# Layer norms on VectorE alone, summed in pairs, and the MLP's gate as a task of its own, in a two-layer decoder step

## The chip, the core and the metric

The kernel runs on one core of a Trainium2 chip. A core has five engines with a queue each: TensorE (PE in the profile; its weight loads are PEld), VectorE (DVE), ScalarE (ACT), GpSimd (POOL) and SyncE (SP), and 16 DMA engines that move data between HBM and the core's memory (SBUF). TensorE writes into eight banks of an accumulator memory (PSUM). The metric is the device time of one execution in microseconds (us); less is better.

## The reference, cut to what matters

One inference step through two decoder layers, for a prompt of 1024 tokens and eight samples of four tokens each: 1056 tokens of 1024 features, all in fp32. Each layer has a mixer (pooling and retention in the first layer, latent attention with a paged cache in the second) and a gated MLP; each of the four is followed by a layer norm over the residual sum. The change touches the norm and the MLP:

```python
def layer_norm(x, g, b):
    mu = jnp.mean(xf, axis=-1, keepdims=True)
    var = jnp.mean(jnp.square(xf - mu), axis=-1, keepdims=True)
    return (xf - mu) * lax.rsqrt(var + LN_EPS) * g + b

def conv_ffn(x, hist, w_up, conv_w, conv_b, w_down):
    h = x @ w_up                         # 1024 -> 2 * 2816
    a, b = h[..., :D_FF], h[..., D_FF:]
    a_ext = jnp.concatenate([hist, a], axis=1)
    conv = conv_b
    for j in range(3):
        conv = conv + conv_w[j] * a_ext[:, j:j + L]
    return (jax.nn.silu(conv) * b) @ w_down, a_ext[:, L:]

# per layer
xp = layer_norm(ALPHA * xp + mixer(xp), ln_mix_g, ln_mix_b)
xp = layer_norm(ALPHA * xp + conv_ffn(xp), ln_ffn_g, ln_ffn_b)
```

## The kernel before, in words

**Layout.** Features lie on the 128 partitions, tokens along the free axis. The residual `z` is [128, 8, 1056]: eight rows of 128 features each. The 1056 tokens are worked in three chunks of 352 (`CHUNKS`); the very last stage has four chunks of 352, 288, 256 and 160 (`ENDS`).

**Matrix products.** A product in fp32 is made of three faster ones. Each operand is split into a high part (a cast to fp32r, on ScalarE) and a low part (the operand less its high part): for weights `wh` and `wl`, 128x1024 elements a unit, for activations `xh` and `xl` (x in the profile), for the gate's result `ah` and `al`. `mm3` multiplies high with high, high with low and low with high. A block (`block`) is one output tile of 128 features by one chunk: eight times `mm3`, 24 matmuls, into one bank.

**Weights.** `open_weights` starts two tasks: one loads raw weights from the SP queue into two buffers (`wr`), the other cuts them into four pairs of buffers (`wh`, `wl`). The low half is written by the engine that `pick` chooses out of the unit's list: before, VectorE and GpSimd for nearly all units (`ffn_units`, `out_units`, `mla_units`).

**The layer norm** (`layer_norm`, from line 743) runs once per chunk, thirteen times in all. It sums the eight rows of z, takes the mean over the partitions with one fp32 matmul by a matrix of 1/1024 (`self.mean`), has ScalarE copy the mean from its bank (`ln_m`), subtracts it from two rows at a time, squares (ScalarE, `ln_q`, one row at a time), sums the squares (`ln_v`), takes their mean in the same way, then root (ScalarE), reciprocal (VectorE, `ln_r`), and for each pair of rows multiply, scale and shift (ScalarE or VectorE), high part (ScalarE or VectorE) and low part. For some chunks TensorE does a sum itself with eight matmuls (`SUM1`, `SUM2`, `END1`, `END2`: the last chunk's sum, and in the last stage also the squares of the last two). The steps that a local function `op` issues go to VectorE or GpSimd, whichever the planner believes will finish first, with 1000 ns in VectorE's favour (`LNX`).

**The MLP** (`ffn`): 22 features of 128, in phases (`SIZES`). For each feature and chunk there is a block for the first half (`first`: ScalarE copies it into the row buffer `a`, one of two) and one for the second (`second`: three VectorE steps of the convolution into `y`, Silu on ScalarE, a multiply with the block's bank into `g`, then `split` into `ah` and `al`). `down` multiplies a phase's features by the down weights and adds into z. In the first phase (`head`) the blocks follow chunk by chunk: all four of chunk 0, then chunk 1, then chunk 2, each as the norm before it gets done.

**What sets the order.** Everything is written as Python generators (tasks) with priorities, run by a planner (`Pipe.run`) that keeps estimated clocks of the engines (`Clocks`). A task yields what it waits for: an event, a buffer, data that must be ready (`rd`), or that VectorE's clock is at most 1 us ahead (`lag`). At each step the planner takes the first task by priority whose wait has ended at TensorE's estimated time. Norms have priority 0, the MLP 10, the output projection's blocks 10 to 17 (`out_proj`, `one`, which also adds the block to z after it). The order in which the tasks issue instructions becomes their rank; a scheduler behind it then builds each engine's queue, in which an instruction of lower rank can go ahead of one that is not ready by that scheduler's estimate. Each queue is then worked strictly in its order.

All engine calls pass through one recording helper, so that most lines of the profile are 405 (the other engines), 616 (`mm`), 632 (`tile`) and 638 (`tr`).

Of the kernel before, what the change touches and what calls it, by code (L numbers as in the profile page):

```python
# [7 lines left out]
F32 = mybir.dt.float32  # L8
# [48 lines left out]
LNX = -1000.0  # L57
SX = 400.0
HX = 0.0
# [502 lines left out]
class Kernel:  # L562
# [180 lines left out]
    def layer_norm(self, c, g, b, event, final=None, chunks=CHUNKS):  # L743
# [13 lines left out]
        for k in range(8):  # L757
# [3 lines left out]
            if c in sum1:  # L761
                if pm is None:
                    pm = yield from self.bank()
                yield ("rd", z[:, k])
                self.mm(pm[:, :n], self.mean, z[:, k], k == 0, k == 7)
            elif k:
                if s1 is None:
                    s1 = self.ln.tile([128, n], F32, tag="ln_s", name="ln_s", bufs=2)
                op(s1, z[:, 0] if k == 1 else s1, z[:, k], ALU.add)
        if pm is None:  # L770
            yield ("rd", s1)
            pm = yield from self.bank()
            self.mm(pm[:, :n], self.mean, s1, True, True)
        mc = self.ln.tile([128, n], F32, tag="ln_r", name="ln_m", bufs=2)
        nc.scalar.copy(mc, pm[:, :n])
        self.drop()
        prev = pv = None
        for i in range(0, 8, 2):
            op(z[:, i:i + 2], z[:, i:i + 2], wide(mc), ALU.subtract)
            for k in range(i, i + 2):  # L780
                sq = self.ln.tile([128, n], F32, tag="ln_q", name="ln_q", bufs=2)
                nc.scalar.activation(sq, z[:, k], AF.Square)
                if c in sum2:
                    if pv is None:
                        pv = yield from self.bank()
                    yield ("rd", sq)
                    self.mm(pv[:, :n], self.mean, sq, k == 0, k == 7)
                else:
                    if k == 0:
                        s2 = self.ln.tile([128, n], F32, tag="ln_s", name="ln_v", bufs=2)  # L790
# [8 lines left out]
        rs = self.ln.tile([128, n], F32, tag="ln_r", name="ln_r", bufs=2)  # L799
        nc.scalar.activation(rs, pv[:, :n], AF.Sqrt, bias=self.eps[:, 0:1])  # L800
        nc.vector.reciprocal(rs, rs)
        self.drop()
        for i in range(0, 8, 2):
            yield ("lag", "dve")
            zz = z[:, i:i + 2]
            op(zz, zz, wide(rs), ALU.mult)
            for k in range(i, i + 2):
# [4 lines left out]
            if final is None:  # L812
                hi = self.xh[:, i:i + 2, t0:t0 + n]
                if self.soonest([zz], {"act": 94.0 + n / 0.6, "dve": HX + 70.0 + n / 0.96}, (nc.scalar, nc.vector)) is nc.scalar:
                    nc.scalar.copy(hi, zz)
                else:
                    nc.vector.tensor_copy(hi, zz)
                op(self.xl[:, i:i + 2, t0:t0 + n], zz, hi.bitcast(F32), ALU.subtract)
            else:
                final(c, i, i + 2)  # L820
        pipe.give("ln", at=pipe.now)
# [55 lines left out]
    def ffn_units(self, l):  # L877
        both = (self.nc.vector, self.nc.gpsimd)
# [18 lines left out]
    def ffn(self, l, src, ln, event, final=None):  # L897
# [28 lines left out]
        def second(f, c, ps):  # L926
# [12 lines left out]
            nc.scalar.activation(y[:, :w], y[:, :w], AF.Silu)  # L939
            g = fp.tile([128, CH], F32, tag="g", name="g")  # L940
# [107 lines left out]
    def out_units(self, key, src):  # L1048
        both = (self.nc.vector, self.nc.gpsimd)
# [965 lines left out]
```

## Time and profile before

| | us |
|---|---|
| median of 3 runs | 2903.41 (2899.09 to 2904.54) |
| profiled execution, its own time | 2902.8 |
| its span, first to last instruction | 2901.0 |
| TensorE busy in the span | 2743.6 |
| mean granted TensorE clock | 0.97 |

The stages, from the span's start: retention and pooling to about 341 us, the output projection to about 445, the first MLP to about 1240, latent attention's projections to about 1412, its attention to about 1966, its output projection to about 2072, the second MLP to the end. The norms lie at the seams, around 395 to 495, 1180 to 1260, 2030 to 2123, and 2808 to the end.

How to read the rows: a timeline row has start, duration, engine, line, operation, output<-inputs, shape (partitions x elements), how many are merged, and in brackets the idle time of the engine before it and what released it. A row of waits has the total, the number of times and the longest. A group row has busy time, mean ns of one, and the idle time before. The granted clock is a share of TensorE's full speed.

### The profile page before, as it was taken

Reading aid. Unit: us, or ns where it says so; the run is one execution under the profiler, and the core shown is the slowest. Engines: PE = TensorE matmul, PEld = TensorE weight load, DVE = VectorE, ACT = ScalarE, POOL = GpSimd, SP = SyncE. Lnnn points to the kernel's source line nnn. Section 1 sums busy time; section 2 is a strip of 40 time slices with the busy share of each in tenths; the row PEclk is TensorE's granted clock in tenths of the full one; section 3 lists DMA queues with packets and bytes.
Section 4 is the critical chain, followed back from the end, with each engine's and each line's share of the span. In section 5 each row is a group of like instructions: output and inputs, shape, how many; then the busy total and the mean of one; then the engine's idle time right before and its main releaser. Section 6 shows DMA issues by size and latency. Waiting matters only on the chain.

```text
span 2901.0 us, 43639 instructions
## 1 busy us (share of the span) xinstructions
PE 2743.6 (95%) x16897; PEld 2459.3 (85%) x16897; DVE 1417.1 (49%) x2721; ACT 867.5 (30%) x1831; POOL 850.1 (29%) x884
## 2 busy tenths in 40 slices
PE   8999998999999999989888989799899999999997
PEld 6777997999999999879745555469789999999996
DVE  4444547544444444774343535355764444444455
ACT  3323435211211222243233433243431211211223
POOL 1222334010110010333577777643410110011112
PEclk9999999999999999999999999899999999999997
DMA  3111420211111111132888999874211111111101
GB/s 137 60 56 50 118 80 23 65 44 37 59 44 38 58 44 52 38 100 67 254 293 280 310 318 314 274 236 140 66 44 37 59 44 33 63 45 46 49 25 60
DMA packets 127055, 301.78 MB, mean 104 GB/s; under 512 B 20960, under 2 KB 71952, under 8 KB 126720
## 3 DMA queue, kind: packets, MB, share of 16 engines
q1 hardware_dynamic: 75648, 159.62, 16.9%
q0 software_dynamic: 32576, 113.73, 11.5%
q10 hardware_dynamic: 18624, 25.63, 3.0%
q8 instruction: 134, 2.20, 0.3%
q14 instruction: 73, 0.60, 0.1%
HBM read 283.71 MB, written 15.21 MB: 103 GB/s over the span
## 4 chain that ended last, share of the span: by engine, by line
PE 77%; DMA 6%; DVE 5%; issue 5%; POOL 4%; ACT 2%; SPq 0%; POOLq 0%; DVEq 0%; ACTq 0%
PE bank L616 70%; PE bank L632 3%; DMA kt<-in_kT,kix 3%; DMA vt<-in_vrow,vix 2%; PE sc L616 2%; POOL kt L405 2%; PE bank L638 1%; DVE x L405 1%; DVE ln_v L405 1%; DVE z L405 1%; POOL z L405 1%; DMA p<-qpd 1%; DVE wl L405 1%; DMA kt<-in_kT 1%; POOL vt L405 0%
## 5 line engine op out<-in xcount | busy, mean ns | idle before, releaser
L616 PE MATMUL bank<-x,wh 128*128 128x352 f32 x5664 | 1379.7, 326 | 18.1 <-DVE x L405 16.6
L616 PEld LDWEIGHTS bank<-x,wh 128*128 128x128 f32 x5664 | 992.8, 190 | 32.7 <-DVE x L405 21.7
L616 PE MATMUL bank<-x,wl 128*128 128x352 f32 x2832 | 915.7, 324 | 9.4 <-DVE wl L405 9.4
L616 PEld LDWEIGHTS bank<-x,wl 128*128 128x128 f32 x2832 | 537.1, 190 | 11.1 <-DVE wl L405 10.6
L405 ACT CAST wh<-wr 128x1024 fp32r<-128x1024 f32 (+1 forms) x196 | 202.7, 1041 | 669.9 <-PE bank L616 638.6
L405 DVE SCALAR_TENSOR_TENSOR z<-z,bank 128x352 f32<-128x352 f32 (+3 forms) x440 | 219.6, 511 | 325.6 <-PE bank L616 319.6
L616 PE MATMUL bank<-ah,wh 128*128 128x352 f32 (+3 forms) x1088 | 352.8, 324 | 0.0
L616 PE MATMUL bank<-ah,wl 128*128 128x352 f32 (+3 forms) x1088 | 350.3, 322 | 0.0
L616 PE MATMUL bank<-al,wh 128*128 128x352 f32 (+3 forms) x1088 | 350.2, 322 | 0.0
L405 POOL TENSOR_TENSOR wl<-wr,wh 128x1024 fp32r<-128x1024 f32 (+1 forms) x60 | 145.3, 2430 | 638.3 <-PE bank L616 391.6
L405 POOL DMA_INDIRECT kt<-in_kT,kix x256 | 252.1, 985 | 84.3 <-issue 59.9
L405 DVE TENSOR_TENSOR wl<-wr,wh 128x1024 fp32r<-128x1024 f32 (+1 forms) x138 | 176.9, 1284 | 147.9 <-ACT wh L405 143.3
L616 PE MATMUL bank<-wh,x 128*128 128x512 f32 (+3 forms) x720 | 238.7, 393 | 8.1 <-ACT wh L405 8.1
L616 PEld LDWEIGHTS bank<-ah,wh 128*128 128x128 f32 x1088 | 207.6, 191 | 1.3 <-issue 0.2
L616 PEld LDWEIGHTS bank<-al,wh 128*128 128x128 f32 x1088 | 207.4, 191 | 1.4 <-issue 0.2
L616 PEld LDWEIGHTS bank<-ah,wl 128*128 128x128 f32 x1088 | 207.5, 191 | 0.6 <-DVE wl L405 0.6
L405 POOL COPY co<-a 128x2 f32<-128x2 f32 x44 | 39.2, 892 | 553.9 <-ACT a L405 553.9
L405 DVE SCALAR_TENSOR_TENSOR y<-a,prm,y 128x352 f32<-128x352 f32 (+1 forms) x264 | 166.1, 629 | 9.8
L405 DVE TENSOR_TENSOR g<-y,bank 128x352 f32<-128x352 f32 (+2 forms) x176 | 71.5, 427 | 202.2 <-PE bank L616 201.1
L405 DVE TENSOR_SCALAR y<-a,prm 128x352 f32<-128x352 f32 x132 | 77.0, 583 | 183.6 <-ACT a L405 178.1
L616 PEld LDWEIGHTS bank<-wh,x 128*128 128x128 f32 (+1 forms) x720 | 127.6, 181 | 32.5 <-ACT wh L405 8.1
L405 POOL DMA_INDIRECT vt<-in_vrow,vix x128 | 125.8, 983 | 72.8 <-PE bank L632 28.1
(234 smaller groups left out, 3184.4 us busy)
## 6 DMA issues: line engine op xcount, KB each, us to landing
wr<-in_w_up SPq DMA_DIRECT2D x88, 512.0 KB
kt<-in_kT SPq DMA_DIRECT2D x256, 160.0 KB
wr<-in_w_dn SPq DMA_DIRECT2D x44, 512.0 KB
wr<-in_w_h SPq DMA_DIRECT2D x16, 512.0 KB
wr<-in_w_oe SPq DMA_DIRECT2D x16, 512.0 KB
wr<-in_w_om SPq DMA_DIRECT2D x16, 512.0 KB
z<-in_xT SPq DMA_DIRECT2D x12, 352.0 KB
z<-in_xT ACTq DMA_DIRECT2D x3, 1408.0 KB
```

What stands on the lines that cost most here:

```text
L405: r = f(*args, **kw)
L616: self.nc.tensor.matmul(out, lhsT, rhs, start=start, stop=stop)
L632: self.nc.tensor.matmul(out[32 * g:32 * g + m], lhsT, rhs, start=start, stop=stop, tile_position=(0, 32 * g))
L638: self.nc.tensor.transpose(out, in_, self.ident[:in_.shape[0], :in_.shape[0]])
```

## The change

In the norm, sums run over pairs of rows (tiles of [128, 2, n], one pair added to the next), so that the two halves of a pair are added by two accumulating matmuls with `self.mean`. The subtraction reads the mean straight from the bank; the copy `ln_m` is gone. Squares are taken two rows at a time, and the adds of squares come one pair later. All these steps, and multiply and low part, are VectorE's; the high part is always ScalarE's; the low part of a pair is issued after the next pair's multiply. The low halves of weights, other than the first mixer's and two units that GpSimd cuts whole, are VectorE's. In the MLP, `second` becomes a task of priority 3 that waits for the Silu and for the cast before it issues the next VectorE step; a feature's first block waits until the gate of the feature two before it is done.

```diff
@@ layer_norm
-        both = (nc.vector, nc.gpsimd)
-
-        def op(out, x, y, alu):
-            w = int(np.prod(out.shape[1:]))
-            self.pick(both, w, x, y, more=LNX).tensor_tensor(out, x, y, alu)
+        op = nc.vector.tensor_tensor
...
-            elif k:
+            elif k > 1 and k % 2:
                 if s1 is None:
-                    s1 = self.ln.tile([128, n], F32, tag="ln_s", name="ln_s", bufs=2)
-                op(s1, z[:, 0] if k == 1 else s1, z[:, k], ALU.add)
+                    s1 = self.ln.tile([128, 2, n], F32, tag="ln_s", name="ln_s", bufs=3)
+                op(s1, z[:, 0:2] if k == 3 else s1, z[:, k - 1:k + 1], ALU.add)
         if pm is None:
             yield ("rd", s1)
             pm = yield from self.bank()
-            self.mm(pm[:, :n], self.mean, s1, True, True)
-        mc = self.ln.tile([128, n], F32, tag="ln_r", name="ln_m", bufs=2)
-        nc.scalar.copy(mc, pm[:, :n])
-        self.drop()
+            for a in range(2):
+                self.mm(pm[:, :n], self.mean, s1[:, a], a == 0, a == 1)
         prev = pv = None
+        sqs = []
         for i in range(0, 8, 2):
-            op(z[:, i:i + 2], z[:, i:i + 2], wide(mc), ALU.subtract)
-            for k in range(i, i + 2):
-                sq = self.ln.tile([128, n], F32, tag="ln_q", name="ln_q", bufs=2)
-                nc.scalar.activation(sq, z[:, k], AF.Square)
-                if c in sum2:
...
-                    else:
-                        op(s2, prev, sq, ALU.add)
-                    prev = s2 if k else sq
+            op(z[:, i:i + 2], z[:, i:i + 2], wide(pm[:, :n]), ALU.subtract)
+            if len(sqs) == 2:
+                op(sqs[1], sqs[0], sqs[1], ALU.add)
+                del sqs[0]
+            if i == 6:
+                self.drop()
+            sq = self.ln.tile([128, 2, n], F32, tag="ln_s", name="ln_q", bufs=3)
+            nc.scalar.activation(sq, z[:, i:i + 2], AF.Square)
+            if c in sum2:
...
+                for a in range(2):
+                    self.mm(pv[:, :n], self.mean, sq[:, a], i + a == 0, i + a == 7)
+            else:
+                sqs.append(sq)
             yield ("lag", "dve")
         if pv is None:
-            yield ("rd", s2)
+            op(sq, sqs[0], sq, ALU.add)
+            yield ("rd", sq)
             pv = yield from self.bank()
-            self.mm(pv[:, :n], self.mean, s2, True, True)
+            for a in range(2):
+                self.mm(pv[:, :n], self.mean, sq[:, a], a == 0, a == 1)
...
+        low = []
         for i in range(0, 8, 2):
             yield ("lag", "dve")
             zz = z[:, i:i + 2]
             op(zz, zz, wide(rs), ALU.mult)
+            if low:
+                op(*low.pop())
...
-                if self.soonest([zz], {"act": 94.0 + n / 0.6, "dve": HX + 70.0 + n / 0.96}, (nc.scalar, nc.vector)) is nc.scalar:
-                    nc.scalar.copy(hi, zz)
-                else:
-                    nc.vector.tensor_copy(hi, zz)
-                op(self.xl[:, i:i + 2, t0:t0 + n], zz, hi.bitcast(F32), ALU.subtract)
+                nc.scalar.copy(hi, zz)
+                low.append((self.xl[:, i:i + 2, t0:t0 + n], zz, hi.bitcast(F32), ALU.subtract))
@@ ffn_units, out_units and mla_units alike
-        both = (self.nc.vector, self.nc.gpsimd)
+        both = (self.nc.vector,)
@@ ffn: second
             nc.scalar.activation(y[:, :w], y[:, :w], AF.Silu)
+            yield ("rd", y)
...
-            self.split(ah[:, t0:t0 + n], al[:, t0:t0 + n], g)
+            nc.scalar.copy(ah[:, t0:t0 + n], g)
+            yield ("rd", ah[:, t0:t0 + n])
+            nc.vector.tensor_tensor(al[:, t0:t0 + n], g, ah[:, t0:t0 + n].bitcast(F32), ALU.subtract)
             self.pipe.fire(("act", l, f, c))
@@ ffn: piece
             u = yield from self.unit(("up", l, f, j))
+            if j == 0 and c == 0 and f > 1:
+                yield ("ev", ("act", l, f - 2, 2))
             ps = yield from self.block(u, ks, c, xs)
-            (first, second)[j](f, c, ps)
+            if j:
+                self.pipe.add(second(f, c, ps), 3)
+            else:
+                first(f, c, ps)
```

More of the change, by code (lines that the diff above doesn't have):

```diff
@@ L772, in layer_norm @@
             pm = yield from self.bank()
-            self.mm(pm[:, :n], self.mean, s1, True, True)
-        mc = self.ln.tile([128, n], F32, tag="ln_r", name="ln_m", bufs=2)
-        nc.scalar.copy(mc, pm[:, :n])
-        self.drop()
+            for a in range(2):
+                self.mm(pm[:, :n], self.mean, s1[:, a], a == 0, a == 1)
         prev = pv = None
+        sqs = []
         for i in range(0, 8, 2):
-            op(z[:, i:i + 2], z[:, i:i + 2], wide(mc), ALU.subtract)
-            for k in range(i, i + 2):
-                sq = self.ln.tile([128, n], F32, tag="ln_q", name="ln_q", bufs=2)
-                nc.scalar.activation(sq, z[:, k], AF.Square)
-                if c in sum2:
[L784 to L787, printed above, removed]
-                else:
-                    if k == 0:
-                        s2 = self.ln.tile([128, n], F32, tag="ln_s", name="ln_v", bufs=2)
-                    else:
-                        op(s2, prev, sq, ALU.add)
-                    prev = s2 if k else sq
+            op(z[:, i:i + 2], z[:, i:i + 2], wide(pm[:, :n]), ALU.subtract)
[7 more added lines that the diff above has]
+            if c in sum2:
+                if pv is None:
+                    pv = yield from self.bank()
+                yield ("rd", sq)
[3 more added lines that the diff above has]
+                sqs.append(sq)
@@ L794, in layer_norm @@
             yield ("lag", "dve")
         if pv is None:
-            yield ("rd", s2)
+            op(sq, sqs[0], sq, ALU.add)
+            yield ("rd", sq)
             pv = yield from self.bank()
-            self.mm(pv[:, :n], self.mean, s2, True, True)
-        rs = self.ln.tile([128, n], F32, tag="ln_r", name="ln_r", bufs=2)
+            for a in range(2):
+                self.mm(pv[:, :n], self.mean, sq[:, a], a == 0, a == 1)
+        rs = self.ln.tile([128, n], F32, tag="ln_r", name="ln_r", bufs=1)
@@ L813, in layer_norm @@
                 hi = self.xh[:, i:i + 2, t0:t0 + n]
-                if self.soonest([zz], {"act": 94.0 + n / 0.6, "dve": HX + 70.0 + n / 0.96}, (nc.scalar, nc.vector)) is nc.scalar:
-                    nc.scalar.copy(hi, zz)
-                else:
-                    nc.vector.tensor_copy(hi, zz)
-                op(self.xl[:, i:i + 2, t0:t0 + n], zz, hi.bitcast(F32), ALU.subtract)
+                nc.scalar.copy(hi, zz)
+                low.append((self.xl[:, i:i + 2, t0:t0 + n], zz, hi.bitcast(F32), ALU.subtract))
             else:
                 final(c, i, i + 2)
+        if low:
+            op(*low.pop())
         pipe.give("ln", at=pipe.now)
@@ L1048, in out_units @@
     def out_units(self, key, src):
-        both = (self.nc.vector, self.nc.gpsimd)
+        both = (self.nc.vector,)
         return [((key, p, ob), src[ob], 1024, both) for p in range(2) for ob in range(8)]
@@ L1283, in mla_units @@
         io = self.io
-        e = (self.nc.vector, self.nc.gpsimd)
+        e = (self.nc.vector,)
         out = [(("dq", i), io["w_dq"][i], 1024, e) for i in range(4)]
```

2 lines of the change are left out of this document (removed).

## The prediction, made before the changed kernel was run

> **What bounds the kernel now.** I read the page's first part, then a table of stretches, then the list of waits of TensorE, then the timelines around the largest waits.
>
> ```profile
> PE 2743.6 (95%) x16897; PEld 2459.3 (85%) x16897; DVE 1417.1 (49%) x2721; ACT 867.5 (30%) x1831; POOL 850.1 (29%) x884
> ```
>
> TensorE is the bound by far, so a change to the other engines can gain only where TensorE stands still or runs slowly. The stretches show where. Their columns are the length, then busy time (count) of PE, PEld, DVE, ACT and POOL, the granted clock, and DMA.
>
> ```profile
> 395.00:495.00 100.00, 82.34 (x440) 75.62 (x438) 73.31 (x80) 49.43 (x80) 47.53 (x24) 0.93 0.16 53
> 495.00:1180.00 685.00, 684.89 (x4285) 684.61 (x4286) 311.06 (x551) 152.79 (x275) 72.33 (x104) 1.00 0.15 48
> 1180.00:1260.00 80.00, 62.73 (x349) 57.64 (x349) 67.88 (x80) 28.13 (x49) 38.87 (x22) 0.96 0.19 65
> 2030.00:2123.00 93.00, 76.85 (x404) 70.80 (x402) 71.14 (x76) 48.27 (x77) 44.38 (x22) 0.91 0.16 51
> 2808.00:2901.00 93.00, 72.39 (x428) 67.69 (x427) 55.45 (x94) 31.15 (x67) 23.45 (x16) 0.80 0.14 47
> 2893.00:2901.00 8.00, 0.00 (x0) 0.00 (x0) 3.13 (x6) 3.17 (x8) 0.00 (x0) 0.63 0.26 83
> ```
>
> The body of an MLP (the second row; that of the other layer is like it) has TensorE busy 684.9 of 685.0 us at full clock. Nothing is to be had there. The other rows are the four places with layer norms; I call them m0, f0, m1 and f1, after the events in the code. There TensorE stands idle 17.7, 17.3, 16.2 and 20.6 us, the last with an 8.0 us tail after the last matmul. What it waited for, over the whole span (total, times, longest):
>
> ```profile
> PE bank L632 <- DMA vt<-in_vrow,vix: 36.8, 19, 8.9
> PE bank L616 <- DVE ln_v L405: 28.4, 11, 4.2
> PE bank L616 <- DVE x L405: 16.6, 12, 3.2
> PE bank L616 <- DVE wl L405: 9.4, 3, 7.1
> PE bank L616 <- DVE z L405: 6.8, 4, 2.7
> ```
>
> The first row is attention's, which the change leaves alone. The next ones are the layer norms: the sum of squares (ln_v) that TensorE must add over partitions, the normalised x that the next matmuls read, and low halves of weights (wl) queued behind such work.
>
> **Why the norms are late.** Here are VectorE's operations of 704 elements, and GpSimd's row of the same time.
>
> ```profile
> 471.29 2.39 DVE L405 TENSOR_TENSOR x<-z,x 128x704 fp32r<-128x704 f32 x1
> 473.60 2.01 DVE L405 CAST x<-z 128x704 fp32r<-128x704 f32 x1
> 475.97 0.88 DVE L405 TENSOR_TENSOR x<-z,x 128x704 fp32r<-128x704 f32 x1
> ```
> ```profile
> 468.86 6.37 POOL L405 TENSOR_TENSOR z<-z,ln_m 128x704 f32<-128x704 f32 x3 [3.26 <-ACT ln_m L405]
> ```
> ```profile
> L405 POOL TENSOR_TENSOR z<-z,ln_m 128x704 f32<-128x704 f32 x30 | 65.3, 2202 | 66.1 <-ACT ln_m L405 66.1
> L405 POOL TENSOR_TENSOR z<-z,ln_r 128x704 f32<-128x704 f32 x30 | 57.6, 1945 | 74.5 <-DVE ln_r L405 74.5
> L405 POOL TENSOR_TENSOR wl<-wr,wh 128x1024 fp32r<-128x1024 f32 x59 | 143.7, 2445 | 624.8 <-PE bank L616 391.6 <-ACT wh L405 233.1
> ```
>
> While GpSimd ran (until 475.2), the same subtraction took VectorE 2.39 us that took 0.88 once GpSimd was done. GpSimd itself takes 2.2 us for such a step. So a step given to GpSimd costs its chain 2.2 us in place of 0.9, and costs VectorE about 1.5 us for nothing. The 60 norm steps in these two groups are what moves back.
>
> **Part 1: the norm on VectorE, in pairs.** I work out one chain, chunk 1 of m0.
>
> ```profile
> 439.30 0.75 PE L616 MATMUL bank<-ln_s,mean 128*128 128x352 f32 x2
> 451.47 1.54 PE L616 MATMUL bank<-ln_v,mean 128*128 128x352 f32 x2 [2.83 <-DVE ln_v L405]
> 462.64 0.76 PE L616 MATMUL bank<-z,mean 128*128 128x352 f32 x2
> 466.04 0.42 PE L616 MATMUL bank<-x,wh 128*128 128x352 f32 x1 [2.65 <-DVE x L405]
> 480.96 0.86 PE L616 MATMUL bank<-ln_v,mean 128*128 128x352 f32 x2 [2.02 <-DVE ln_v L405]
> 494.17 0.59 PE L616 MATMUL bank<-x,wh 128*128 128x352 f32 x2 [3.12 <-DVE x L405]
> ```
> ```profile
> 440.08 0.45 ACT L405 COPY ln_m<-bank 128x352 f32<-128x352 f32 x1 [1.73 <-PE bank L616]
> 461.80 1.25 ACT L405 ACTIVATE z<-z,prm 128x352 f32<-128x352 f32 x2 [0.51 <-POOL z L405]
> 464.76 0.76 ACT L405 CAST x<-z 128x704 fp32r<-128x704 f32 x1
> 483.25 0.56 ACT L405 ACTIVATE ln_r<-bank,eps 128x352 f32<-128x352 f32 x1
> ```
> ```profile
> 455.71 2.35 DVE L405 RECIPROCAL ln_r<-ln_r 128x352 f32<-128x352 f32 x1
> ```
>
> Before: from the matmul of the mean (439.30) to the first usable x (466.04) 26.7 us. After, with 0.88 us a step of 704: two mean matmuls 1.2 (their price is below); four subtractions and three adds 6.2, and the last square, at most the 0.76 of the cast, 6.9 in all; two matmuls 1.2; root 0.6; reciprocal 2.35; then multiply 0.9, scale 1.25, cast 0.76, subtract 0.9. That is 16.1 us, plus perhaps 0.1 us at each of ten hand-overs, 17. Between them VectorE also has to place gate steps and weight halves, some 4 to 5 us. So 21 to 22 us, where TensorE has 26.7 - 2.83 - 2.65 = 21.2 us of other work. The wait is gone, or about 1 us. The later pairs follow at ScalarE's pace, 1.25 + 0.76 = 2.0 us each.
>
> For chunk 2 the mean's last matmul stands at 462.64 and the first x at 494.17, 31.5 us. Its chain overlaps the end of chunk 1's, so I leave 3 us of wait there. With small rests elsewhere I leave 7 us idle in each of m0 and m1: gains of 10.7 and 9.2 us. In f0 part of the waiting is for weights that can be cut only when the last down block has freed their buffers, and for their loads; I leave 9 of 17.3: 8.3 us. In f1 the chains hide under 288- and 256-wide blocks; I leave 5 of the 12.6 that are not tail: 7.6 us. The tail loses the copy of the mean, and four squares instead of eight: 1.5 us.
>
> **What it adds.** Each sum of a pair needs two mean matmuls where one was needed.
>
> ```profile
> 396.68 0.32 PE L616 MATMUL bank<-x,wl 128*128 128x352 f32 x1
> 396.83 0.77 PE L616 MATMUL bank<-ln_s,mean 128*128 128x352 f32 x2
> ...
> 397.75 0.32 PE L616 MATMUL bank<-x,wl 128*128 128x352 f32 x1
> ...
> 398.24 0.32 PE L616 MATMUL bank<-x,wl 128*128 128x352 f32 x1
> ```
>
> From one such low matmul to the next it is 0.49 us, and 1.07 with the mean between them: 0.58 us for each. The code takes the means by VectorE's sums nine times and the variances eleven times in the thirteen norms, so 20 more: five each in m0, f0 and m1, 2.9 us apiece, and five narrower ones (1536 columns together) in f1, 2.5 us. That is 11.2 us where it lies under TensorE's other work; bounds 0 (all in waits) and 11.2. I take 11.2, since I remove the waits.
>
> The subtraction now reads the mean from PSUM. Rows of the MLP's body bound it:
>
> ```profile
> L405 DVE TENSOR_TENSOR al<-g,ah 128x352 fp32r<-128x352 f32 x63 | 32.8, 521 | 11.1 <-ACT ah L405 11.1
> L405 DVE TENSOR_TENSOR g<-y,bank 128x352 f32<-128x352 f32 x41 | 21.4, 521 | 54.2 <-PE bank L616 54.2
> L405 DVE TENSOR_TENSOR wl<-wr,wh 128x1024 fp32r<-128x1024 f32 x44 | 53.9, 1225 | 59.4 <-ACT wh L405 59.4
> ```
>
> With one operand from PSUM or none it is 521 ns: no cost. [...]
>
> **The clock.** A wait costs twice, because the granted clock falls behind it.
>
> ```profile
> 2859.00:2870.00 11.00, 10.41 (x43) 9.64 (x43) 9.58 (x12) 4.24 (x9) 5.83 (x4) 0.50 0.15 54
> 482.00:484.00 2.00, 2.00 (x9) 2.00 (x8) 0.65 (x2) 1.99 (x3) 0.00 (x0) 0.50 0.00 0
> ```
>
> In m0, f0, m1 and f1 the mean clocks 0.93, 0.96, 0.91 and 0.80 are 7.0, 3.2, 8.4 and 18.6 us of full speed lost, some of it while idle. I take back about half in the first three (3.5, 1.5 and 4 us), since about half of the waiting goes, and a third in f1 (6 us), where the tail holds part of it. The bounds are 0 and the sum of the four, 37 us.
>
> [...]
>
> **Part 2: weights' low halves on VectorE alone.** GpSimd's 59 (less two that the code keeps there) at VectorE's 1.225 us are 70 us more for VectorE over the whole span. Even if all fell into one MLP body, VectorE would be busy 383 of 685 us there, and TensorE waits for nothing: no cost. In m0 GpSimd's 24 operations, 20 norm steps and four halves, become some 23 us of VectorE's, against the stretched parts of its own that it loses. No DMA moves, and GpSimd's queue only gets shorter.
>
> **Part 3: the gate as a task.** Its multiply no longer stands at the head of VectorE's queue until the Silu is done, nor its subtraction until the cast is. In the bodies that is free. In the four stages it lets norm steps past, which is counted above. The new wait of a feature for the gate two before it holds up only that feature's own blocks, behind six blocks of 24 matmuls at 0.49 us for three, 23 us, against a gate of some 4 us; the bank that the gate holds longer is one of eight. Price 0; if the cover were gone, a wait would stand in the bodies, 40 times.
>
> **Sum**, against the profiled execution's own 2902.8 us (span 2901.0; the median of the runs, 2903.4, is 0.6 more): m0 -10.7 - 3.5 + 2.9 = -11.3; f0 -8.3 - 1.5 + 2.9 = -6.9; m1 -9.2 - 4 + 2.9 = -10.3; f1 -7.6 - 6 - 1.5 + 2.5 = -12.6. Together -41.1: 2862 us, and as much for the median to within its 0.6.
>
> **Rivals.** First, the third norm starts late.
>
> ```profile
> 443.42 0.51 DVE L405 SCALAR_TENSOR_TENSOR z<-z,bank 128x352 f32<-128x352 f32 x1
> ```
>
> Its last row of z is there at 443.93, but its mean's last matmul comes at 462.64, behind all blocks of chunk 0, because the task that ends the last output block has a lower priority than the MLP and gets its turn only when the MLP waits. If chunk 1's norm is now finished before that point, the MLP waits for nothing, and this matmul may slip behind the blocks of chunk 1 too. Then a whole chain of 17 us stands open in m0 and m1, some 14 us more than I left in each: -41.1 + 28 = -13.1, 2890 us. My chain ends within 1 us of that point, so this is open: 0.2.
>
> Second, slower: VectorE becomes the bound in the norms. If its rows in m0 do not shrink once GpSimd is silent, 73.3 + 23 us in 100 leave no room; the waits stay at their old lengths, and the 11.2 us of matmuls come on top, with some 5 us of queueing: 2919 us. It decides from the point where VectorE's busy share in m0 is above nine tenths. The rows at 471.29 and 475.97 speak against it: 0.07.
>
> Third, no change: VectorE's and ScalarE's queues give back two thirds of the waits' gain, and the matmuls take the rest; about 2902 us: 0.05.
>
> **How the numbers follow.** The forecast, with 0.68, is 2862 us; its own range, 2840 to 2882, comes from idle rests of half or one and a half times what I left and from a clock that recovers wholly or hardly. A measurement of this kernel can tell about 0.2%, 5.8 us. Faster by more: the forecast and most of the late third norm, 0.84. Within: 0.08. Slower: 0.08. For eight in ten the range goes from 2838 to 2897 us, leaving out the slower case and the thin ends.
>
> **What would show it.** GpSimd's norm groups are gone, and VectorE's steps of 704 take 0.9 us throughout. The ln_v waits (28.4 us) fall below 8, the waits for x (16.6) below 8. Mean clock in f1 is above 0.88. The bodies stay at 684.9 of 685. I would be wrong if an x wait of over 10 us stands after chunk 1 in m0 (first rival), if VectorE is above nine tenths busy there (second), or if waits appear in the bodies.

## The result, and the profile after

The changed kernel takes 2839.99 us, the median of four runs (2837.62 to 2841.46), against 2903.97 us before: a ratio of 0.9781, 95% interval 0.9764 to 0.9798, 64 us less. The profiled execution took 2838.57 us, its span 2836.8 us. The prediction was 2862 us, in a range of 2838 to 2897: the direction was right, the gain half as large again as forecast, which puts the time within 2 us of the range's lower end.

The page's first part, after:

```profile
PE 2726.0 (96%) x16937; PEld 2448.0 (86%) x16937; DVE 1418.8 (50%) x2752; ACT 872.7 (31%) x1794; POOL 560.2 (20%) x745
```

GpSimd (POOL) lost 290 us of work, and VectorE (DVE) took most of it over, yet VectorE's busy time rose by 1.7 us. Part of the room came from 24 casts of the high part, which are ScalarE's now. They had taken VectorE 28.3 us:

```profile
L405 DVE CAST x<-z 128x704 fp32r<-128x704 f32 x24 | 28.3, 1182 | 6.3 <-ACT z L405 6.3
```

The rest came mostly from its own stretched steps, as the run with the norm alone shows below without that help. TensorE does 40 matmul records more (the 20 means) in 17.6 us less.

TensorE's waits after (total, times, longest); the lines left out are those of attention and of the cutting of weights by ScalarE:

```profile
...
PE bank L614 <- ACT x L403: 5.4, 4, 1.6
PE bank L614 <- DVE z L403: 4.5, 3, 2.2
...
PE bank L614 <- DVE x L403: 3.1, 4, 1.1
...
PE bank L614 <- DVE wl L403: 2.1, 2, 1.1
...
PE bank L614 <- ACT ln_q L403: 1.1, 1, 1.1
```

The largest wait of before, 28.4 us for the sums of squares, has no successor but the 1.1 us for ln_q. The waits for x fell from 17.7 us (16.6 behind VectorE, 1.1 behind ScalarE) to 8.5 in two rows, those for weights' low halves from 9.4 to 2.1.

To see where the 64 us came from, I cut both executions at the same events: from the last matmul of pooling to the first down block (m0), from there to the first matmul of attention's scores (f0, with the first MLP's body in it), from the end of attention to the next first down block (m1), and from there to the end (f1). The rows have length, busy time (count) of PE, PEld, DVE, ACT and POOL, granted clock, DMA. Before:

```profile
342.40:511.90 169.50, 151.74 (x864) 145.02 (x864) 98.17 (x124) 66.43 (x105) 67.02 (x40) 0.95 0.26 82
511.90:1419.00 907.10, 885.17 (x5504) 873.85 (x5502) 441.78 (x749) 228.92 (x440) 160.92 (x171) 0.99 0.19 61
1965.40:2139.80 174.40, 156.95 (x891) 150.43 (x891) 116.14 (x149) 78.19 (x130) 64.17 (x37) 0.94 0.26 87
2139.80:2901.00 761.20, 740.59 (x4620) 735.58 (x4618) 356.42 (x627) 175.59 (x328) 93.54 (x113) 0.98 0.15 47
```

After:

```profile
343.25:492.38 149.13, 145.10 (x874) 140.01 (x873) 96.61 (x128) 67.03 (x96) 1.86 (x8) 1.00 0.29 93
492.38:1386.20 893.82, 885.05 (x5515) 874.36 (x5514) 444.04 (x764) 234.46 (x436) 63.93 (x127) 1.00 0.19 62
1931.00:2086.80 155.80, 151.34 (x901) 146.16 (x902) 108.79 (x152) 78.74 (x121) 1.61 (x6) 0.99 0.28 96
2086.80:2836.80 750.00, 736.02 (x4629) 732.12 (x4628) 364.37 (x636) 174.21 (x312) 26.79 (x80) 0.99 0.15 47
```

Length less PE's busy time is TensorE's idle time. It fell from 17.8 to 4.0 us in m0, from 21.9 to 8.8 in f0, from 17.5 to 4.5 in m1, and from 20.6 to 14.0 in f1. Busy time fell too, although there is more to do: in m0 by 6.6 us with ten records more, at a clock of 1.00 where it was 0.95. So the same matmuls ran faster.

| us, after less before | m0 | f0 | m1 | f1 | sum |
|---|---|---|---|---|---|
| idle, measured | -13.7 | -13.2 | -13.0 | -6.6 | -46.5 |
| idle, predicted (the tail's 1.5 with f1) | -10.7 | -8.3 | -9.2 | -9.1 | -37.3 |
| busy, measured | -6.6 | -0.1 | -5.6 | -4.6 | -16.9 |
| busy, predicted (clock and means) | -0.6 | +1.4 | -1.1 | -3.5 | -3.8 |

The rest of the span (everything up to m0, and attention) differs by 0.8 us.

### The profile page after: what moved, and what is told of

Same layout as the page of the kernel before. It is cut to its first block, busy times and chain, and to the rows that moved or that the text cites. A ratio compares the mean times of both kernels' runs of the same rounds, so it can differ in the third digit from the quotient of the medians.

```text
span 2836.8 us, 43462 instructions
## 1 busy us (share of the span) xinstructions
PE 2726.0 (96%) x16937; PEld 2448.0 (86%) x16937; DVE 1418.8 (50%) x2752; ACT 872.7 (31%) x1794; POOL 560.2 (20%) x745
## 3 DMA queue, kind: packets, MB, share of 16 engines
q0 software_dynamic: 32576, 113.73, 11.8%
## 4 chain that ended last, share of the span: by engine, by line
PE 86%; DMA 6%; DVE 3%; issue 2%; POOL 2%; ACT 1%; SPq 0%; ACTq 0%; POOLq 0%; DVEq 0%
PE bank L614 78%; PE bank L630 4%; PE sc L614 3%; DMA vt<-in_vrow,vix 2%; PE bank L636 2%; DMA kt<-in_kT,kix 2%; DMA p<-qpd 1%; DVE z L403 1%; POOL kt L403 1%; DMA kt<-in_kT 0%; DVE ln_r L403 0%; POOL u L403 0%; DVE amx L403 0%; ACT z L403 0%; DMA wr<-in_w_h 0%
## 5 line engine op out<-in xcount | busy, mean ns | idle before, releaser
L614 PE MATMUL bank<-x,wh 128*128 128x352 f32 x5664 | 1365.2, 324 | 11.2 <-ACT x L403 5.4
L614 PEld LDWEIGHTS bank<-x,wh 128*128 128x128 f32 x5664 | 982.0, 188 | 22.8 <-ACT x L403 5.9
L403 DVE TENSOR_TENSOR wl<-wr,wh 128x1024 fp32r<-128x1024 f32 (+1 forms) x196 | 237.8, 1216 | 166.1 <-ACT wh L403 158.0
L403 DVE SCALAR_TENSOR_TENSOR y<-a,prm,y 128x352 f32<-128x352 f32 (+1 forms) x264 | 155.6, 589 | 10.3
L614 PE MATMUL bank<-wl,x 128*128 128x512 f32 (+3 forms) x360 | 137.6, 382 | 0.0
L403 DVE TENSOR_SCALAR y<-a,prm 128x352 f32<-128x352 f32 x132 | 61.5, 466 | 142.0 <-ACT a L403 136.5
```

What stands on the lines that cost most here:

```text
L403: r = f(*args, **kw)
L614: self.nc.tensor.matmul(out, lhsT, rhs, start=start, stop=stop)
```

## The experiments

My theory, "GpSimd" below, is the prediction's: GpSimd's steps are slow (2.2 us each) and stretch VectorE's beside them (2.39 us where 0.88 was taken without them), and that is where the time went. The rivals are "pairs" (the wider steps and the mean from the bank shortened the chain) and "gate" (the gate had blocked VectorE's queue).

The runs were made on several chips. On some of them attention takes 673 to 693 us instead of 545, with TensorE waiting there, and f0 has one wait of 4 to 16 us more in attention's projections, in kernels with and without the change. For the same kernel (the repeat of the kernel after, below) m0, m1 and f1 agree within 2 us, and f0 within 3.4 us once that wait is taken off: at its end the first run of the kernel after waits 3.4 us for a transfer of `kt`, before attention's first matmul, which some of the other runs do and some do not. So each kernel is compared by its ratio to the kernel before on its own chip, and by its stages, each from one profile; for f0 the wait of 4 to 16 us stands in brackets.

| kernel | m0 | f0 | m1 | f1 | ratio, 95% interval |
|---|---|---|---|---|---|
| before | 169.5 | 907.1 | 174.4 | 761.2 | 1 |
| after | 149.1 | 893.8 | 155.8 | 750.0 | 0.9781 (0.9764 to 0.9798) |
| after again | 150.4 | 900.4 (10.0) | 154.2 | 751.8 | 0.9796 (0.9773 to 0.9819) |
| norm on VectorE only | 151.8 | 900.2 (7.8) | 157.5 | 748.4 | 0.9805 (0.9789 to 0.9821) |
| weights on VectorE only | 170.5 | 914.8 (9.2) | 175.0 | 760.2 | 1.0005 (0.9993 to 1.0018) |
| gate only | 169.5 | 914.5 (9.2) | 175.1 | 758.6 | 1.0000 (0.9988 to 1.0012) |
| all but the pairs | 150.4 | 911.9 (16.4) | 156.9 | 747.9 | 0.9788 (0.9772 to 0.9805) |
| after, no gate task | 151.9 | 899.5 (9.2) | 153.9 | 749.8 | 0.9788 (0.9767 to 0.9809) |
| after, mean copied | 152.2 | 889.1 | 159.0 | 746.2 | 0.9769 (0.9752 to 0.9785) |
| after, narrow idle work | 156.5 | 899.6 (10.0) | 163.1 | 776.4 | 0.9932 (0.9916 to 0.9949) |
| after, wide idle work | 161.6 | 899.7 | 167.4 | 750.0 | 0.9873 (0.9856 to 0.9889) |
| after, one mean matmul | 151.0 | 887.1 (4.3) | 155.0 | 742.4 | 0.9718 (0.9702 to 0.9734) |
| and no sum on TensorE | 145.8 | 888.9 | 151.0 | 742.4 | 0.9729 (0.9713 to 0.9746) |
| and high part on either | 148.9 | 898.7 | 156.5 | 742.4 | 0.9774 (0.9758 to 0.9791) |

### One part of the change at a time

The norm's steps on VectorE, nothing else:

```diff
-        both = (nc.vector, nc.gpsimd)
-        def op(out, x, y, alu):
-            w = int(np.prod(out.shape[1:]))
-            self.pick(both, w, x, y, more=LNX).tensor_tensor(out, x, y, alu)
+        op = nc.vector.tensor_tensor
```

> The kernel before, with the norm's steps on VectorE alone and nothing else of the change. Theory GpSimd (the waits of TensorE in the norms come from GpSimd's 2.2 us steps and from VectorE's steps that last 2.39 us beside them): more than half of the 64 us comes, about 2865 us; the ln_v waits (28.4 us) fall below 12, and VectorE's busy time in the first norm stage does not grow by what it takes over. Theory pairs (the gain comes from fewer, wider steps and from the mean read in its bank): VectorE now has fifteen single steps more for each norm, the chain is no shorter: 2895 to 2915 us. Theory gate (the gate's multiply and subtraction blocked VectorE's queue): about 2900 us, the ln_v waits stay above 20.

Measured: 2983.01 us against 3040.59 on that chip, 58 us less. VectorE's page line and one of its groups:

```profile
PE 2774.2 (93%) x16897; PEld 2469.3 (83%) x16897; DVE 1413.8 (47%) x2812; ACT 852.6 (29%) x1818; POOL 693.0 (23%) x802
```
```profile
L405 DVE TENSOR_TENSOR z<-z,ln_m 128x704 f32<-128x704 f32 x40 | 34.3, 886 | 12.9 <-ACT ln_m L405 12.9
```

In the kernel before the same subtraction stood at:

```profile
L405 DVE TENSOR_TENSOR z<-z,ln_m 128x704 f32<-128x704 f32 x10 | 13.1, 1311 | 10.1 <-ACT ln_m L405 10.1
```

VectorE does 91 instructions more than in the kernel before, twelve of them casts that ScalarE had done, and it is busy 3 us less: 40 subtractions of 704 at 886 ns, where ten took it 1311 ns on average and 30 took GpSimd 2202. The waits for ln_v fell to 3.4 us; those for x did not fall (20.2 us, 7.7 at the longest). By stages against the gate-only kernel of the same chip, which is as long as before, it is 17.7, 14.3, 17.6 and 10.2 us. This one edit brings nearly all of the gain; theory pairs and theory gate are out as its main cause.

The low halves of weights on VectorE, nothing else (`both` becomes `(self.nc.vector,)` in three lists of units):

> The kernel before, with the low halves of weights on VectorE alone and nothing else of the change. Theory GpSimd: most of the 57 operations lie in the MLP's bodies, where nothing waits; only where they stand beside norms does it help: the wl waits (9.4 us) go, 2893 to 2903 us. Theory pairs and theory gate: 2898 to 2909 us. A rival: in the norms GpSimd goes on stretching VectorE's steps, and VectorE now has the weights too: 2910 us or more.

Measured: nothing, 3041.65 us against 3040.59. The wait for ln_v stayed, and the rival's 2910 us did not come either:

```profile
PE bank L616 <- DVE ln_v L405: 27.5, 11, 4.0
```

I had expected the wl waits to go. They did not (9.9 us against 9.4), so what held them was not that GpSimd cut some of them; with the norm's steps alone on VectorE one wl wait of 1.1 us was left in f0.

The gate as a task, nothing else (the last two blocks of the change's diff):

> The kernel before, with the gate as a task that waits for its results, and nothing else of the change. Theory GpSimd and theory pairs: within 6 us of 2904 us, the waits for ln_v and x as before (28.4 and 16.6 us). Theory gate: 2885 us or less, the ln_v waits below 15. The recorded step of the prediction was that this part is worth nothing by itself in the bodies and only lets norm steps past in the norm stages.

Measured: nothing, 3040.8 us against 3040.59, ln_v waits 27.4 us; those for x were 22.7, not the 16.6 that I had expected. And taken out of the kernel after again (the end of the edit; the waits for the Silu, for the cast and for the gate two features before go too):

```diff
-            if j:
-                self.pipe.add(second(f, c, ps), 3)
-            else:
-                first(f, c, ps)
+            (first, second)[j](f, c, ps)
```

> The kernel after, with the gate's steps issued at once again instead of as a task. Theory GpSimd: within 6 us of the kernel after, as the gate as a task alone moved nothing on the kernel before. Theory gate in company (with GpSimd silent VectorE's queue is the next limit, and the gate at its head stops norm steps): 8 us or more slower, with the waits for x and ln_q in the two first norm stages above 10 us in sum each.

> The kernel after, unchanged, beside the next three on one chip. The runs of the norm and the weights alone were on a chip on which latent attention took some 130 us longer, and there the same absolute gain is a smaller ratio. All theories: if this chip is like the first, 0.978 again; on one like the second 0.979 to 0.980; the norm stages as before, 149.1 us from the retention's end to the first down block, 155.8 us in the second layer.

Measured beside each other on one chip: 2987.35 us without the gate task, 2993.57 with it, the intervals overlapping almost wholly. The gate task is worth nothing in company either.

All of the change but the pairs (the old sums, with norm, weights and gate as after):

> The kernel after, but with the norm's old sums (single rows, the mean copied, squares one row at a time, the high part on ScalarE or VectorE, the low part at once): norm steps and weights on VectorE alone, and the gate as a task. Theory GpSimd: within 10 us of the kernel after, 2830 to 2850 us; 20 matmuls of a mean fewer (11 us) against a longer chain. Theory pairs: 2875 us or more, and the ln_v waits stay above 15 us. Theory gate: near the kernel after too, but then the gate alone would have given most.

Measured: ratio 0.9788, the same as the kernel after within the intervals. Its stages but f0, where that chip's own wait is 16.4 us, are within 2.1 us. So the norm's new form, with its pairs, two matmuls for each mean, no copy and the high part on ScalarE, adds up to nothing that these runs can tell from zero. The runs with one mean matmul and with the high part on either engine, below, show that this is a sum of gains and losses.

### Is it GpSimd's slowness or what it does to VectorE?

Both could be the reason: GpSimd's own step of 2.2 us in the chain, or the stretched steps of VectorE. To separate them I gave GpSimd work in the kernel after that no one waits for. First:

```diff
+            if i == 0:
+                nc.gpsimd.tensor_tensor(dum, sq[:, :, :56], ones[1], ALU.add)
+                for _ in range(37):
+                    nc.gpsimd.tensor_tensor(dum, ones[0], ones[1], ALU.add)
```

> The kernel after, plus 38 additions of 112 elements on GpSimd in each of the thirteen norms, which start when the norm's first square is there and whose result nobody reads. Theory stretch (what GpSimd's work cost was the lengthening of VectorE's steps beside it): VectorE's steps of 704 elements last over 1.5 us in the norms, and 20 us or more of the gain are lost, 2860 us or more on the first chip (ratio 0.985 or more). Theory chain (what it cost was the 2.2 us of its own steps inside the chain): nobody waits for these additions, so the time stays within 6 us of the kernel after.

Measured: 3033.7 us against 2993.57 of the kernel after on that chip, 40 us lost. But the run mixes causes. GpSimd fell behind in f1, where the span now ends with its last additions, and its first addition read a buffer that ScalarE needed again. Waits of ScalarE, in the last stage:

```profile
ACT ln_q L403 <- POOL ln_d L403: 16.3, 2, 9.1
```

So only m0 and m1 say something, 6.1 and 8.8 us longer than in the kernel after on that chip. Beside these narrow additions VectorE's two-operand steps of 704 in m0 took 0.88 to 1.13 us, most of them 1.1, not the 1.5 that I had expected. The second try reads constants, is wider, and leaves f1 alone:

```diff
+            if i == 0 and final is None:
+                nc.gpsimd.tensor_copy(dum[:, 0:4], z[:, 0, 0:4])
+                for _ in range(22):
+                    nc.gpsimd.tensor_tensor(dum, *two, ALU.add)
```

> The kernel after, plus 22 additions of 224 elements of constants on GpSimd in each norm of m0, f0 and m1 (none in f1), started by a copy of four elements of z when the first square is issued; nobody reads the result. In the run with 38 narrow additions ScalarE's squares waited 16.3 us in f1 for a buffer that GpSimd's first, queued addition still read, so that its loss mixed two causes; here no ring buffer is read. Theory stretch: VectorE's steps of 704 elements with both inputs in SBUF last 1.1 us or more (0.88 before), those with the mean from the bank stay at 0.88; m0 and m1 become 5 to 12 us longer each, f1 stays at 750 us from the first down block to the end. Theory chain: m0, f0 and m1 stay within 2 us of those of the kernel after (149 to 150, 894, 154 to 156 us), as no step of a norm is GpSimd's.

Measured: 2867.91 us, 28 us of the gain lost. m0 is 12.5 us longer, f0 5.9, m1 11.6, and f1, which has no such work, 750.0 as after. In m0 GpSimd is busy 65.7 us, as long as before (67.0), with no step in any chain. The other engines' work there is that of the kernel after: 873 records against 874 on TensorE, 126 instructions against 128 on VectorE, 96 on ScalarE in both. So another order of the queues, which an edit to `op` can also bring, is hardly the cause. A stretch of VectorE's timeline in m0, and GpSimd's at that time:

```profile
441.52 0.87 DVE L403 TENSOR_TENSOR z<-z,bank 128x704 f32<-128x704 f32 x1
442.31 1.30 DVE L403 TENSOR_TENSOR ln_q<-ln_q 128x704 f32<-128x704 f32 x1
443.54 0.87 DVE L403 TENSOR_TENSOR z<-z,bank 128x704 f32<-128x704 f32 x1
444.34 1.30 DVE L403 TENSOR_TENSOR ln_q<-ln_q 128x704 f32<-128x704 f32 x1
445.57 0.81 DVE L403 TENSOR_SCALAR y<-a,prm 128x352 f32<-128x352 f32 x1
```
```profile
439.83 20.63 POOL L403 TENSOR_TENSOR ln_d<-prm 128x224 bf16<-128x224 f32 x22
```

The subtraction that reads the mean from its bank takes 0.87 us, as in the kernel after (0.88); the addition of two operands in SBUF, of the same size, takes 1.30 in the same stretch, and the gate's first step 0.81 where it takes 0.46 on average after. The groups over the whole execution, which take in f1 without idle work, say the same:

```profile
L403 DVE TENSOR_TENSOR z<-z,ln_r 128x704 f32<-128x704 f32 x40 | 40.5, 1029 | 0.1
...
L403 DVE TENSOR_TENSOR ln_q<-ln_q 128x704 f32<-128x704 f32 x30 | 36.0, 1200 | 3.7 <-ACT ln_q L403 3.3
...
L403 DVE TENSOR_TENSOR z<-z,bank 128x704 f32<-128x704 f32 x40 | 33.9, 878 | 11.1 <-PE bank L614 11.1
```

Theory stretch holds: idle work alone gives back 12.5 of m0's 20.4 us and 11.6 of m1's 18.6. That the rest is GpSimd's own pace in the chain is argued, not shown; its operations here were also shorter than before's. That the place of one operand, in SBUF (1.30 us) or in a bank (0.87), makes the difference is my reading of these rows: no run moves it alone beside idle work. Why the gate's first step, with one tensor and a column of parameters as inputs, went to 0.81 is not separated here either.

### What the norm's new form costs and brings

The mean copied to SBUF again, as before:

```diff
+        mc = self.ln.tile([128, n], F32, tag="ln_r", name="ln_m", bufs=1)
+        nc.scalar.copy(mc, pm[:, :n])
+        self.drop()
...
-            op(z[:, i:i + 2], z[:, i:i + 2], wide(pm[:, :n]), ALU.subtract)
+            op(z[:, i:i + 2], z[:, i:i + 2], wide(mc), ALU.subtract)
```

> The kernel after, but ScalarE copies the mean out of its bank again (0.45 us, as before) and the subtractions read the copy. The prediction's step (an operand in PSUM costs the subtraction nothing): the subtraction stays at 0.88 us, and the copy adds 0.45 us and a hand-over to thirteen chains: 0 to 8 us slower than the kernel after. Rival (the operand from PSUM costs): the subtraction of 704 falls below 0.82 us and the time is equal or less.

Measured: 2837.81 us, the same as the kernel after. m0 and m1 are 3 us longer each, which fits the copy in their chains; f0 and f1 are 5 and 4 us shorter. In f0, 3.4 us of it is the wait for `kt`, which this run does not have; for f1 I have no shown cause. The subtraction:

```profile
L403 DVE TENSOR_TENSOR z<-z,ln_m 128x704 f32<-128x704 f32 x40 | 33.8, 886 | 12.7 <-ACT ln_m L403 12.7
```

It takes 886 ns from SBUF and 882 ns from the bank in the kernel after.

One matmul for each mean:

```diff
-            for a in range(2):
-                self.mm(pm[:, :n], self.mean, s1[:, a], a == 0, a == 1)
+            op(s1[:, 0], s1[:, 0], s1[:, 1], ALU.add)
+            self.mm(pm[:, :n], self.mean, s1[:, 0], True, True)
```

and the same for the squares.

> The kernel after, but VectorE adds the two halves of a pair sum (128x352, some 0.45 us), and one mean matmul follows in place of two: 20 matmuls less. The prediction's step (0.58 us each, 11.2 us, where they lie under other work of TensorE): 6 to 11 us faster than the kernel after. Rival one: the added step lies on the chain of every norm and gives it back, within 4 us of the kernel after. Rival two: it is slower by more than 4 us, since the chain sets the end of a wait in most norms.

Measured: 2971.17 us against 2993.57 on that chip, 22 us less; of this 5.7 are that chip's own wait in f0 (10.0 against 4.3). By the four stages and without that wait it is 15.7 us against the repeat on that chip (m0 +0.5, f0 -7.6, m1 +0.8, f1 -9.4) and 13.2 us against the first run of the kernel after (m0 +1.9, f0 -6.7, m1 -0.8, f1 -7.6). The sum is near the predicted 11.2, but the place is not: m0 and m1 bring nothing, and f1 gives three times its share or more. There the doubled matmuls had cost more than their own time. A wait and the clock of the kernel after in its last stage:

```profile
2807.19 0.54 PE L614 MATMUL bank<-z,mean 128*128 128x160 f32 x2 [2.16 <-DVE z L403]
```
```profile
2811.00:2814.00 3.00, 3.00 (x13) 0.50 0.01 3
```

(The last row: length, PE's busy time, granted clock, DMA.) Behind a wait of 2.16 us TensorE ran at half clock. With one mean matmul the stretch before the last matmul has waits of 1.1 and 0.5 us only, and the clock stays at 1.00 to the end of it. TensorE's busy time in f1 is 8.9 us less than in the first run of the kernel after, where it was busy for 11.8 us at half clock: 5.9 us are the clock's, and 3.0 are left for the matmuls, near the predicted 2.5.

Taking TensorE's own sums of the third chunk away too (`SUM1 = (2,)` becomes `SUM1 = ()`):

> The kernel with one mean matmul, and VectorE also sums the rows of the third chunk in pairs (SUM1 empty), where TensorE did it with eight matmuls: 21 matmuls less in m0, f0 and m1 together. At 0.58 us each that is 12 us of TensorE; the third chunk's chain grows by one addition of 0.88 and one of 0.52 us at its start, less the last of the eight matmuls. Theory TensorE-bound (each matmul taken off TensorE is time): 6 to 12 us faster than the one-mean kernel, ratio 0.968 to 0.970. Rival (the third norm's chain sets the end of m0 and m1): equal within 4 us, with longer x waits.

Measured: 2824.83 us. By stages it is 5.2 us shorter than the one-mean kernel in m0 and 4.0 in m1, f0 1.8 longer, f1 equal: 7.4 us. It is the fastest by stages, and beats the kernel after by 15 us (2839.99, on a chip with the same time before). By the whole time it is not shown to beat the one-mean kernel: the expected ratio of 0.968 to 0.970 did not come, 0.9729 stands against 0.9718, and each gain over the kernel before on its own chip is 79 and 85 us. By the stages, the matmuls taken off TensorE in m0 and m1 are time, and there the third chunk's sums hide.

At last, the high part of a pair on whichever of ScalarE and VectorE the planner picks, as before the change:

```diff
-                nc.scalar.copy(hi, zz)
+                if self.soonest([zz], {"act": 94.0 + n / 0.6, "dve": 70.0 + n / 0.96}, (nc.scalar, nc.vector)) is nc.scalar:
+                    nc.scalar.copy(hi, zz)
+                else:
+                    nc.vector.tensor_copy(hi, zz)
```

> The kernel with SUM1 empty and one mean matmul, in which the high part of a pair may again go to VectorE when the planner believes that it is done earlier there (VectorE's cast of 704 elements against ScalarE's 0.76 us). There TensorE still waits 11.0 us for x from ScalarE, 4.7 us at the longest. Theory ScalarE's pace (scale and cast of a pair, 2.0 us, set the third norm): these waits fall to 6 us or less, 2 to 6 us faster. Rival (the third norm is late before its first pair, by the fold of the squares behind a gate step and by ScalarE's table loads): within 3 us, the waits as before.

Measured: 2837.49 us, 12.7 us slower; a miss of the expectation, and outside the rival's 3 us too. All 36 casts went to VectorE, and the waits for x doubled. By stages it is 3.2, 9.8 and 5.5 us longer in m0, f0 and m1, and the same in f1; attention was 3.9 us shorter in this run. In the kernel with no sum on TensorE, and in this one:

```profile
PE bank L614 <- ACT x L403: 11.0, 4, 4.7
```
```profile
PE bank L614 <- DVE x L403: 23.3, 7, 7.6
```
```profile
L403 DVE CAST x<-z 128x704 fp32r<-128x704 f32 x36 | 18.6, 521 | 0.7 <-ACT z L403 0.6
```

A cast takes VectorE 0.52 us and ScalarE 0.77, so each went to where it is shorter; but the low part and the next pair's steps stand in VectorE's queue behind the cast (how that makes the wait is argued, the wait itself is shown). The change's rule "high part always on ScalarE" is worth some 13 us here, and it is of the size that the doubled means cost.

## Why the prediction was right, and where its sizes were off

**What bounds it, and the bodies: right.** The body of the first MLP is as busy as before at full clock, and in m0 GpSimd's 47.5 us are gone:

```profile
395.00:495.00 100.00, 95.97 (x566) 90.88 (x565) 79.14 (x104) 59.83 (x88) 1.86 (x8) 1.00 0.21 69
495.00:1180.00 685.00, 684.99 (x4295) 684.27 (x4294) 322.07 (x565) 146.81 (x262) 26.41 (x78) 1.00 0.15 46
```

VectorE's busy time in that hundred rose by 5.8 us only, not by 23 (six casts of before, 8.9 us, are ScalarE's now). The second rival needed nine tenths.

**The cause, GpSimd beside VectorE: right**, by the norm alone and by the idle work. VectorE's steps of 704 take 0.9 us throughout:

```profile
L403 DVE TENSOR_TENSOR z<-z,ln_r 128x704 f32<-128x704 f32 x40 | 34.7, 884 | 0.0
L403 DVE TENSOR_TENSOR z<-z,bank 128x704 f32<-128x704 f32 x40 | 34.2, 882 | 11.4 <-PE bank L614 11.2
L403 DVE TENSOR_TENSOR x<-z,x 128x704 fp32r<-128x704 f32 x36 | 31.8, 885 | 2.6 <-ACT x L403 2.5
```

**The chain of chunk 1: right in sum.** Predicted 21 to 22 us from the mean to the first x, the low part included. TensorE's rows after:

```profile
436.58 1.34 PE L614 MATMUL bank<-ln_s,mean 128*128 128x352 f32 x4
447.32 1.34 PE L614 MATMUL bank<-ln_q,mean 128*128 128x352 f32 x4
454.70 0.75 PE L614 MATMUL bank<-z,mean 128*128 128x352 f32 x2
456.46 0.74 PE L614 MATMUL bank<-x,wh 128*128 128x352 f32 x3 [1.01 <-ACT x L403]
458.01 0.43 PE L614 MATMUL bank<-x,wh 128*128 128x352 f32 x1 [0.80 <-DVE x L403]
467.93 1.35 PE L614 MATMUL bank<-ln_q,mean 128*128 128x352 f32 x4
476.01 0.91 PE L614 MATMUL bank<-x,wh 128*128 128x352 f32 x4 [1.64 <-ACT x L403]
```

The first high part is used at 456.46, 19.9 us after 436.58, and the first low part at 458.01, after 21.4 us; the waits there are 1.0 and 0.8 us. One term was missing, ScalarE's change of tables between the gate's Silu and the norm's root:

```profile
446.67 1.28 ACT L403 ACT_TABLE_LOAD   x1 [2.59 <-DVE y L403]
447.96 0.50 ACT L403 ACTIVATE y<-y 128x352 f32<-128x352 f32 x1
448.47 1.28 ACT L403 ACT_TABLE_LOAD   x1
449.77 0.55 ACT L403 ACTIVATE ln_r<-bank,eps 128x352 f32<-128x352 f32 x1
```

The root starts 1.1 us after its matmuls end at 448.66, for which I had set a hand-over of 0.1. With the predicted steps of 17 us and this 1.0, 3.4 us are left for other work between the steps, a little less than the 4 to 5 that I had set.

**The idle time left: mis-sized in m0, f0 and m1.** I left 7 us in m0 and 7 in m1; 4.0 and 4.5 stayed. Most of it is the third norm: it was left 3 us, and 1.64 and 0.58 came. Its mean ends at 455.45 instead of 463.40 and its x follows 21.3 us after the matmul at 454.70, where it had been 31.5. The first rival (this matmul slips behind chunk 1's blocks) did not happen; it came 8 us earlier. In f0 13.2 us went where I had 8.3: the waits for ln_v, z and ln_s there, 8.8 us, are gone, and those for weights' low halves fell by 7.3, while those for high halves rose by 2.4. That the low halves came earlier because the norm steps ahead of them are shorter is argued. In f1 I was too high, 9.1 against 6.6: the tail after the last matmul stayed at 8.3 us, since the copy and the squares that went lie ahead of that matmul.

**The clock: the term that was most wrong.** I let it give back 15 us, in proportion to the waits: 3.5, 1.5, 4 and 6 us in m0, f0, m1 and f1. By the clock records in the two traces TensorE was busy at half clock for 16.2, 9.7, 17.8 and 26.0 us before, and for 0, 5.3, 3.4 and 11.8 us after. At half clock twelve matmuls took 3.40 us, at full clock fourteen took 2.00 (both rows are below), so half of each difference is what came back: 8.1, 2.2, 7.2 and 7.1, together 24.6 us. (TensorE's busy time fell by 16.9 us, and with the predicted 11.2 us of matmuls added that is 28.) The step that failed is "about half in the first three, since about half of the waiting goes": m0 and m1 gave about twice that.

The loss does not go with the sum of the waits, and not with the length of a single one either. In m0 the rows at 476.01 and after it have waits of 1.64 and 0.58 us. Their twins in m1 of the same execution, and the clock behind each pair, m0 first:

```profile
2068.87 0.91 PE L614 MATMUL bank<-x,wh 128*128 128x352 f32 x4 [1.59 <-ACT x L403]
2070.36 0.66 PE L614 MATMUL bank<-x,wh 128*128 128x352 f32 x1 [0.58 <-DVE x L403]
```
```profile
476.00:478.00 2.00, 1.41 (x7) 1.00 0.00 0
478.00:480.00 2.00, 2.00 (x14) 1.00 0.00 0
2070.40:2073.80 3.40, 3.40 (x12) 0.50 0.00 0
```

The pair cost nothing in m0 and 3.4 us at half clock in m1. In the kernel before, a wait of 2.02 us was followed by half clock (482 to 484) and one of 2.61 us was not:

```profile
1206.90 0.86 PE L616 MATMUL bank<-ln_v,mean 128*128 128x352 f32 x2 [2.61 <-DVE ln_v L405]
```
```profile
1206.00:1208.00 2.00, 1.09 (x5) 1.00 0.00 0
1208.00:1210.00 2.00, 2.00 (x14) 1.00 0.00 0
```

In the traces of the kernels before and after, the changes of the clock lie on a grid of 3.41 us, and the clock follows the idle time within the step before. In m0 the two waits fell into two steps, 1.64 us of idle time in the first; in m1 both fell into one, 2.17 us. Outside attention (1412 to 1966 us before, 1380 to 1931 us after), in the two traces together, each of the 15 steps at full clock with more than 2.05 us of idle time was followed by half clock, 6 of the 11 steps with 1.5 to 2.05 us, and 2 of the 1290 with less. Ten of the 15 are in the kernel before and five in the kernel after. So the fewer and shorter waits of the change mostly stay below 2.05 us in a step, and where a wait of 1.6 us lies on the grid is luck: in the repeat of the kernel after the mean clock was 0.99 in m0 and 1.00 in m1, where the first run had 1.00 and 0.99. A count of such steps, and not a proportion, is what I should have used.

**The means: near in size, 11.2 against 13 to 16 us, wrong in place.** In f1 they cost 7.6 to 9.4 us, not 2.5, mostly through half clock.

**The bank as an operand, the weights and the gate: nothing, as predicted.** 882 against 886 ns; ratios of 1.0005 and 1.0000; and 0.9788 without the gate against 0.9796 with it.

**Not priced at all: the high part always on ScalarE.** The prediction used ScalarE's 0.76 us in the chain and never asked what the choice had cost before, when 24 of the 36 casts were VectorE's at 1182 ns each. It is some 13 us in the version with one mean matmul and no sum on TensorE.

**The signs.** The ln_v waits fell below 8 us, the mean clock over the last 93 us is 0.90 where I had asked for more than 0.88, and no wait of x over 10 us stands in m0; the waits for x, 8.5 us in sum, just missed their 8.

## What to carry to other kernels

Before giving a slow engine part of a fast one's work, look at what its operations do to the fast one's in the same stretch of the timeline: if the same operation has two durations, here 2.39 and 0.88 us, the helper may cost more than it takes. Price short waits of TensorE by how much idle time falls together into one step of the clock's grid (here more than 2.05 us in 3.41 brought half clock each time), not by their sum. When a change has several parts, ask of each whether it pays for itself: here one edit brought nearly all, and of the rest a gain and a loss of some 13 us each hid one another.

## What the runs showed of the hardware

VectorE's subtraction of 704 elements with the mean in a bank took 0.87 us beside GpSimd's wide additions and 0.88 without them; the addition with both operands in SBUF took 1.30 in the same stretch and 0.89 without them. ScalarE's change of tables took 1.28 us, and in the two rows above the next activation started 0.01 and 0.02 us after it. Outside attention the clock fell to half after each of the 15 steps of 3.41 us at full clock in which TensorE stood idle for more than 2.05 us, though waits of 2.61 and 2.87 us in the kernel before, which lay across two steps, left it at 1.00. The kernel before takes 137 and 152 us longer on two of the chips than on the others (3040.59 and 3056.16 us against 2903.97); in the kernel after attention took 544.8 us on one and 693.2 on another, while m0, m1 and f1 agree within 2 us.
